# The twelve pairs of a combined input projection in another order: values, gates and queries first

## Chip, cores and metric

One core of one Trainium2 chip runs the whole program in one launch. The metric is device time in microseconds (us), the median of three runs. Engines are named as the profile names them: PE (TensorE), DVE (VectorE), ACT (ScalarE), POOL (GpSimd), SP (SyncE, which issues most DMA transfers).

## What is computed

Two layers of a streaming encoder for a sequence of 1024 frames, 1024 channels. Each layer normalises its input, makes one projection of it whose columns are shared out to three mixers, joins their outputs in one output projection with a residual add, and ends in a gated feed-forward net (FFN) with a width-3 convolution and another residual add. Cut to the parts around the change:

```python
q, k = rotary(q, pos) * 64 ** -0.5, rotary(k, pos)   # retention: 4 heads, uses q, k, v, g
xbc = silu(causal_dwconv(xbc, conv_w, conv_b))        # SSD: 512 + 2*128 + 2*128 columns, width 4
y_ssd = groupnorm(ssd_scan(xbc, dt) * silu(z))
xc = causal_dwconv(xin, conv_w, conv_b)               # RG-LRU: width 4
r, i = sigmoid(xc @ w_a + b_a), sigmoid(xc @ w_x + b_x)
a = exp(-8 * r * softplus(-lam)); u = sqrt(1 - a * a) * (i * xc)
h_t = a_t * h_(t-1) + u_t                             # a scan over the frames
y_lru = h * gelu(gate)
```

Retention works with a decaying state over chunks, the SSD mixer with a state of 128 per head over chunks; all inputs and outputs are float32.

## The kernel before

Time is cut into two halves of HT = 512 frames; channels lie on the 128 partitions. A product in float32 is made of three products of split numbers: an operand is split into a rounded high part (ACT, a copy) and the rest (DVE, a subtraction, or POOL, an accumulating DMA): `part_split`, lines 235 to 243, for weights, and L206 for the input.

The input projection of a layer has 24 column tiles of 128. Two neighbouring tiles form a *pair* (class Pair), and a pair's two tiles times two halves, four products of 1024 by 128 by 512, are made with seven smaller products of sums and differences (Strassen's scheme in Winograd's form). `prep` (L851) makes the sums of the weights with four operations (L710: a11, s2, a21, a12) and splits the five results. A pair behind the first then has 84 matmuls on L300, 24 in `start` and 60 in `end`, in five groups of twelve; each group ends in additions (L874, L879, L882, L883, L886), of which L890 is the pair's last. L837 is the addition in `start`. In layer 0 the additions of `start` are followed by L847 and L848, a multiplication by the norm's factors. In front, L744 to L750 are the normalising multiplications of the input itself.

`ORDER` (line 46) names the twelve pairs of a layer in the order in which they are made; both layers use it. A name such as x:6 is a kind and the first tile of the pair. `products` (L895) makes the first pair with `lead` and `follow`, starts the next two early, while the input is still being normalised and split, and then makes one pair after another. Small products for the step sizes dt (L413 is a DVE operation in it) follow pair 1 and pair 3. When a part of a pair is ready, `take` in `in_pair` (L938) hands it on:

- x (four pairs: x:0, x:2, x:4, x:6): `xbc` (L387), a convolution (L315 on ACT, three L318 on DVE), a tanh on ACT, L393, and a store to DRAM;
- z (two pairs) and g: `silu2` (L340), a tanh on ACT and L344 on DVE, and a store;
- v: a store alone;
- q and k: `rotate` (L372), four small DMAs that swap rows (L377) and two that load tables (L381, tile tb), L382, L383, L384 on DVE, and a store;
- lru (two pairs): the first tile goes through `gelu2` (L331, DVE L335, L336, L338), the second through `lru` (L346): a convolution, two gate products on PE (tile lgp, L353), tanh, exp and a square root on ACT (L354 to L360; tables are exchanged for the square root), DVE's L359 and L361, POOL's L362, the scan L363, POOL's L366, and a store.

Each step of this list is done four times for a pair (two tiles, two halves), the recurrence of lru twice. While one pair's results are taken, PE makes the next pair.

Behind the last pair come the `mixers` (L634): in eight chunks of 128 frames they load what was stored (L643), run the SSD chunk (L535; L547 and L575 multiply by masks, cumb is a tile of decays that is loaded by L566, L558 and L559 are POOL's products), the retention chunk (L427) and the gates; and then the output projection (tile op, its products also on L300) and the FFN. Weight splits of the output projection (w_o) are also made there.

A scheduling framework lays the instructions into each engine's queue from the order in which the code is written and an estimate of when each can run, so one engine's rows of several pairs are mixed. The queue is then worked through in order.

Of the kernel before, what the change touches and what calls it, by code (L numbers as in the profile page):

```python
# [42 lines left out]

ORDER = tuple((n, int(i)) for n, i in (x.split(":") for x in "q:0 x:6 z:0 x:2 x:4 lru:0 lru:2 z:2 x:0 k:0 g:0 v:0".split()))
PLACE = {"x": 0, "z": 8, "lru": 12, "k": 16, "q": 18, "g": 20, "v": 22}


# [1 line left out]
def hybrid_trunk(  # L51
# [29 lines left out]
    def nm(s):  # L81
        uid[0] += 1
        return f"{s}{uid[0]}"
# [46 lines left out]
    for k in range(2 * KD):  # L130
# [3 lines left out]
        if k in (1, 5):  # L134
            r = wr.tile([P, 2 * HT], F32, tag="wr", name=nm("wr"))
            (sp, act)[(k + 1) % 2].dma_start(r, w_ct[0, PLACE[ORDER[0][0]] + ORDER[0][1] + len(first) - 1])
            first.append(r)
# [800 lines left out]
    def in_pair(l, kind, i, B):  # L938

        g0 = PLACE[kind] + i  # L940
        gl = {}

        def take(m, h, x, then=None):
            if kind == "x":
                xbc(l, h, i + m, x, then)
                return
            if kind == "lru" and m:
                lru(l, h, i // 2, x, gl[h], then)
                return
            x = body(x)  # L950
            if kind in "zg":
                silu2(x)
                keep(l, h, kind, i + m, x)
            elif kind == "v":
                keep(l, h, kind, i + m, x)
            elif kind in "qk":
                rotate(l, h, kind, i + m, x)
            else:
                gelu2(x)
                gl[h] = x  # L960

        return Pair((w_ct[l, g0], w_ct[l, g0 + 1]), B, take)
# [249 lines left out]
    for l in range(DEPTH):  # L1212
# [15 lines left out]

        pairs = [in_pair(l, kind, i, B) for kind, i in ORDER]
        if l:  # L1230
# [181 lines left out]
```

## Time and profile before

| | us |
|---|---|
| runs | 2347.9, 2351.53, 2354.42 |
| median of the runs | 2351.53 |
| the profiled execution's own time | 2346.2 |
| its span in the trace | 2344.4 |
| PE busy | 2174.7 (93%) |
| DVE busy | 1924.6 (82%) |
| ACT busy | 1288.4 (55%) |
| POOL busy | 302.6 (13%) |

Busy times are those of one profiled execution; a line such as L300 is a line of the kernel, and a helper's line stands for all that call it. Layer 0's projection runs from the start to about 342 us, its mixers to 424, layer 1's projection from about 1200 to 1486 and its mixers to 1567.

### The profile page before, as it was taken

Reading aid. Unit: us, or ns where it says so; the run is one execution under the profiler, and the core shown is the slowest. Engines: PE = TensorE matmul, PEld = TensorE weight load, DVE = VectorE, ACT = ScalarE, POOL = GpSimd, SP = SyncE. Lnnn points to the kernel's source line nnn. Section 1 sums busy time; section 2 is a strip of 40 time slices with the busy share of each in tenths; the row PEclk is TensorE's granted clock in tenths of the full one; section 3 lists DMA queues with packets and bytes.
Section 4 is the critical chain, followed back from the end, with each engine's and each line's share of the span. In section 5 each row is a group of like instructions: output and inputs, shape, how many; then the busy total and the mean of one; then the engine's idle time right before and its main releaser. Section 6 shows DMA issues by size and latency. Waiting matters only on the chain.

```text
span 2344.4 us, 31562 instructions
## 1 busy us (share of the span) xinstructions
PE 2174.7 (93%) x10494; PEld 1758.3 (75%) x10494; DVE 1924.6 (82%) x3763; ACT 1288.4 (55%) x2370; POOL 302.6 (13%) x335
## 2 busy tenths in 40 slices
PE   6699988997999999999978989899989999999997
PEld 4477767885788888878866767777668888887787
DVE  7987858779877788999798877696797788789987
ACT  5357637554566556444445674674556665654443
POOL 0012213000222222000001131210002222210000
PEclk9799999999999999999988999999989999999999
DMA  4365687561666666854334638846437666677522
GB/s 173 108 149 134 150 248 233 167 209 48 149 150 148 145 153 152 285 193 137 108 128 123 152 79 235 266 150 208 137 93 164 144 148 148 147 197 254 178 83 73
DMA packets 176147, 371.94 MB, mean 159 GB/s; under 512 B 19440, under 2 KB 31856, under 8 KB 175984
## 3 DMA queue, kind: packets, MB, share of 16 engines
q1 hardware_dynamic: 135760, 297.55, 38.6%
q0 software_dynamic: 37440, 68.17, 17.1%
q10 hardware_dynamic: 2784, 4.20, 0.5%
q8 instruction: 83, 1.36, 0.3%
q14 instruction: 80, 0.66, 0.1%
HBM read 228.22 MB, written 69.27 MB: 127 GB/s over the span
## 4 chain that ended last, share of the span: by engine, by line
PE 65%; DVE 15%; DMA 8%; issue 7%; ACT 3%; SPq 1%; POOL 1%; DVEq 0%; POOLq 0%; ACTq 0%
PE up L300 43%; PE op L300 6%; PE dy L995 5%; PE dx L995 5%; PE dx L1071 2%; DMA ws<-wr 2%; DVE ws L243 2%; DVE bl L206 1%; DVE xb L318 1%; DMA cumb<-cumscr 1%; DMA tb<-in_rope_dram 1%; DMA g<-g1scr 1%; DMA g<-g0scr 1%; DVE g L710 1%; DMA wr<-in_w_ct_dram 1%
## 5 line engine op out<-in xcount | busy, mean ns | idle before, releaser
L300 PE MATMUL up<-bh,ws 128*128 128x512 f32 x3840 | 1228.2, 400 | 76.4 <-ACT ws L236 50.5
L300 PEld LDWEIGHTS up<-bh,ws 128*128 128x128 f32 x3840 | 735.6, 192 | 249.7 <-ACT ws L236 54.0
L300 PE MATMUL up<-bl,ws 128*128 128x512 f32 x1920 | 761.1, 398 | 11.8 <-DVE bl L206 11.7
L236 ACT ACTIVATE ws<-wr 128x512 fp32r<-128x512 f32 x568 | 348.7, 626 | 358.9 <-PE up L300 129.0
L300 PEld LDWEIGHTS up<-bl,ws 128*128 128x128 f32 x1920 | 369.2, 192 | 102.3 <-DVE bl L206 22.4
L241 POOL DMA_DIRECT2D ws<-wr x222 | 197.6, 905 | 1321.5 <-ACT ws L240 1046.0
L243 DVE TENSOR_TENSOR ws<-wr,ws 128x512 fp32r<-128x512 f32 x346 | 236.5, 688 | 61.0 <-ACT ws L236 54.9
L995 PE MATMUL dy<-ws,ws 128*128 128x512 f32 x792 | 192.2, 390 | 3.2 <-ACT ws L236 1.6
L995 PE MATMUL dx<-ws,ws 128*128 128x512 f32 x792 | 190.8, 390 | 2.1 <-ACT ws L236 1.2
L995 PEld LDWEIGHTS dy<-ws,ws 128*128 128x128 f32 x792 | 148.2, 188 | 36.4 <-DVE ws L243 3.3
L995 PEld LDWEIGHTS dx<-ws,ws 128*128 128x128 f32 x792 | 148.4, 188 | 34.1 <-ACT ws L236 2.1
L318 DVE SCALAR_TENSOR_TENSOR fc<-u,smalls,fc 128x512 f32<-128x512 f32 (+2 forms) x176 | 131.0, 748 | 50.6 <-ACT fc L315 49.6
L240 ACT ACTIVATE ws<-ws 128x512 fp32r<-128x512 f32 x260 | 159.8, 626 | 4.6
L300 PE MATMUL op<-yh,ws 128*128 128x512 f32 x512 | 160.5, 394 | 0.2 <-ACT yh L213 0.2
L318 DVE SCALAR_TENSOR_TENSOR fc<-c,smalls,fc 128x512 f32<-128x512 f32 (+2 forms) x176 | 131.2, 745 | 0.7 <-ACT fc L315 0.3
L315 ACT ACTIVATE fc<-c,smalls 128x512 f32<-128x512 f32 x88 | 71.2, 809 | 103.7 <-DVE c L837 101.7
L243 DVE TENSOR_TENSOR ws<-g,ws 128x512 fp32r<-128x512 f32 (+1 forms) x165 | 103.1, 649 | 13.7 <-ACT ws L236 13.5
L236 ACT ACTIVATE ws<-g 128x512 fp32r<-128x512 f32 (+1 forms) x165 | 92.1, 590 | 39.7 <-PE dy L995 13.8
L300 PEld LDWEIGHTS op<-yh,ws 128*128 128x128 f32 x512 | 95.4, 188 | 21.7 <-ACT yh L213 2.1
L300 PE MATMUL op<-yl,ws 128*128 128x512 f32 x256 | 100.3, 394 | 0.0
L710 DVE TENSOR_TENSOR wr<-wr,wr 128x512 f32<-128x512 f32 x64 | 44.9, 702 | 63.0 <-DMA wr<-in_w_up_dram 28.3
L236 ACT ACTIVATE ws<-s 128x512 fp32r<-128x512 f32 x64 | 40.4, 632 | 101.3 <-DVE s L710 92.4
(303 smaller groups left out, 2939.3 us busy)
## 6 DMA issues: line engine op xcount, KB each, us to landing
ws<-wr POOLq DMA_DIRECT2D x222, 256.0 KB, 4.3
wr<-in_w_up_dram SPq DMA_DIRECT2D x96, 512.0 KB, 4.3
wr<-in_w_dn_dram SPq DMA_DIRECT2D x66, 512.0 KB, 3.9
wr<-in_w_ct_dram SPq DMA_DIRECT2D x56, 512.0 KB, 4.7
wr<-in_w_o_dram SPq DMA_DIRECT2D x32, 512.0 KB, 5.1
g0scr<-fc SPq DMA_DIRECT2D x44, 256.0 KB, 3.3
g<-g0scr SPq DMA_DIRECT2D x44, 256.0 KB, 5.8
g1scr<-fc SPq DMA_DIRECT2D x44, 256.0 KB, 2.9
```

The source lines that it names most:

```text
L206: eng.tensor_tensor(lo, src, hi.bitcast(F32), op=ALU.subtract)
L236: act.activation(w[:, 0, :m], raw, AF.Copy)
L240: act.activation(w[:, 1, :m], w[:, 0, :m].bitcast(F32), AF.Copy, scale=-1.0)
L241: pool.dma_start(w[:, 1, :m].bitcast(F32), raw, accum_op=ALU.add)
L243: eng.tensor_tensor(w[:, 1, :m], raw, w[:, 0, :m].bitcast(F32), op=ALU.subtract)
L300: pe.matmul(dst, W(k, a), A(k, b), start=first and i == 0, stop=last and i == n - 1)
L315: act.activation(dst, body(x), AF.Identity, bias=bias, scale=taps(n))
L318: dve.scalar_tensor_tensor(dst[:, o:HT], x[:, HALO - j + o : HALO - j + HT], taps(n - j), dst[:, o:HT], op0=ALU.mult, op1=ALU.add)
L710: eng.tensor_tensor(o, a, b, op=op)
L995: pe.matmul(d[oc], w[:, a, P * oc : P * oc + P], t[:, b], start=not more and i == 0 and k == 0, stop=i == NP - 1 and k == 2, skip_group_ch ...
L1071: pe.matmul(X[oc][:, e], w[x][:, P * oc : P * oc + P], t[:, y, e], start=False, stop=i == NP - 1 and k == 2, skip_group_check=True)
```

## The change

Line 46 gets another order of the same twelve names. Nothing else is edited; the preload of the first pair's weights (line 136) follows the first name by itself.

```diff
@@ -43,7 +43,7 @@
-ORDER = tuple((n, int(i)) for n, i in (x.split(":") for x in "q:0 x:6 z:0 x:2 x:4 lru:0 lru:2 z:2 x:0 k:0 g:0 v:0".split()))
+ORDER = tuple((n, int(i)) for n, i in (x.split(":") for x in "v:0 z:0 g:0 z:2 q:0 x:6 k:0 x:2 lru:0 x:4 x:0 lru:2".split()))
```

The first three pairs, which are made beside the normalising of the input, were q, x:6 and z:0 and are v, z:0 and g; the last three were k, g and v and are x:4, x:0 and lru:2. The two recurrent pairs stood sixth and seventh, and stand ninth and last.

What DVE has in its queue at the front of layer 0, behind the first products of the early pairs. Before (c and qs are q's output and its swapped copy, x and t the input and its sums):

```order
L320 COPY u_407<-c_421 128x3
L710 TENSOR_TENSOR t_752<-x_125,x_93 128x512
L750 SCALAR_TENSOR_TENSOR x_103<-x_103,first,nr_455 128x512
L382 TENSOR_TENSOR c_353<-c_353,tb_566 128x512
L383 TENSOR_TENSOR qs_561<-qs_561,tb_567 128x512
L206 TENSOR_TENSOR bl_755<-t_752,bh_754 128x512
L384 TENSOR_TENSOR c_353<-c_353,qs_561 128x512
L710 TENSOR_TENSOR x_103<-x_103,t_752 128x512
```

The same place now:

```order
L710 TENSOR_TENSOR t_699<-x_125,x_93 128x512
L344 SCALAR_TENSOR_TENSOR c_421<-gt_695,c_421 128x512
L750 SCALAR_TENSOR_TENSOR x_103<-x_103,first,nr_455 128x512
L206 TENSOR_TENSOR bl_702<-t_699,bh_701 128x512
L710 TENSOR_TENSOR x_103<-x_103,t_699 128x512
```

The rotation's three operations are gone from between the input's sums and splits, and one L344 (of z) stands there.

What DVE has in its queue ahead of the last pair's weights in layer 0 (wr and s are the raw weights and their sums, the row that writes s is the s2 subtraction). Before, with g's last additions around v's weights:

```order
L710 TENSOR_TENSOR wr_2622<-wr_2622,wr_2665 128x512
L879 TENSOR_TENSOR u_2564<-u_2490,up_2551 128x512
L710 TENSOR_TENSOR s_2668<-wr_2665,wr_2622 128x512
L882 TENSOR_TENSOR u_2490<-u_2490,up_2567 128x512
L883 TENSOR_TENSOR c_2565<-u_2564,up_2567 128x512
L886 TENSOR_TENSOR u_2490<-u_2490,up_2582 128x512
L890 TENSOR_TENSOR u_2564<-u_2564,up_2600 128x512
L243 TENSOR_TENSOR ws_2670<-s_2668,ws_2670 128x512
```

Now, with x:0's convolutions (xb) around lru:2's weights, all of it behind x:0's L890:

```order
L318 SCALAR_TENSOR_TENSOR xb_2547<-u_2493,smalls,xb_2547 128x509
L320 COPY c_2494<-u_2493 128x3
L837 TENSOR_TENSOR c_2602<-u_2588,up_2575 128x512
L393 SCALAR_TENSOR_TENSOR xb_2525<-u_2414,xb_2525 128x512
L393 SCALAR_TENSOR_TENSOR xb_2547<-u_2493,xb_2547 128x512
L318 SCALAR_TENSOR_TENSOR xb_2556<-c_2494,smalls,xb_2556 128x512
L847 TENSOR_TENSOR c_2602<-c_2602,nr_455 128x512
L318 SCALAR_TENSOR_TENSOR xb_2556<-c_2494,smalls,xb_2556 128x512
L848 TENSOR_TENSOR u_2588<-u_2588,nr_455 128x512
L318 SCALAR_TENSOR_TENSOR xb_2556<-c_2494,smalls,xb_2556 128x512
L335 TENSOR_SCALAR lt_2606<-lt_2606 128x512
L710 TENSOR_TENSOR s_2615<-wr_2612,wr_2564 128x512
```

The s2 subtraction stood four rows ahead of the previous pair's last addition, and stands behind it and behind the three convolutions that follow it.

What DVE has in its queue at the seam from the last pair to the mixers in layer 0 (cbt and cumb are chunk masks and decays of the SSD mixer). Before:

```order
L890 TENSOR_TENSOR u_2717<-u_2717,up_2750 128x512
L547 TENSOR_TENSOR cbt_2790<-cb_2787,mats 128x256
L575 TENSOR_TENSOR cumb_2811<-cumb_2811,cbt_2790 128x512
L575 TENSOR_TENSOR cumb_2828<-cumb_2828,cbt_2790 128x512
L547 TENSOR_TENSOR cbt_2892<-cb_2889,mats 128x256
L575 TENSOR_TENSOR cumb_2913<-cumb_2913,cbt_2892 128x512
```

Now:

```order
L890 TENSOR_TENSOR u_2664<-u_2664,up_2702 128x512
L338 SCALAR_TENSOR_TENSOR u_2588<-lt_2696,u_2588 128x512
L320 COPY c_2665<-u_2664 128x3
L547 TENSOR_TENSOR cbt_2790<-cb_2787,mats 128x256
L318 SCALAR_TENSOR_TENSOR xc_2716<-u_2664,smalls,xc_2716 128x511
L575 TENSOR_TENSOR cumb_2811<-cumb_2811,cbt_2790 128x512
L318 SCALAR_TENSOR_TENSOR xc_2716<-u_2664,smalls,xc_2716 128x510
L575 TENSOR_TENSOR cumb_2828<-cumb_2828,cbt_2790 128x512
L318 SCALAR_TENSOR_TENSOR xc_2716<-u_2664,smalls,xc_2716 128x509
L361 SCALAR_TENSOR_TENSOR xc_2716<-ti_2722,xc_2716 128x512
L318 SCALAR_TENSOR_TENSOR xc_2742<-c_2665,smalls,xc_2742 128x512
L359 SCALAR_TENSOR_TENSOR lv_2730<-u_2664,lv_2730 128x512
```

The masks of chunk 1 (cbt_2892 and its cumb tiles) stood four rows behind the last addition, and stand some twenty rows behind it, with the recurrent pair's operations and some splits of w_o between.

## Rows read from the trace of the kernel before

**Rows 1.** The page, busy time of each engine, share of the span and instructions.

```profile
PE 2174.7 (93%) x10494; PEld 1758.3 (75%) x10494; DVE 1924.6 (82%) x3763; ACT 1288.4 (55%) x2370; POOL 302.6 (13%) x335
```

**Rows 2.** Busy times by stretch; the first line names the columns.

```profile
core 0: us, PE busy (x) PEld busy (x) DVE busy (x) ACT busy (x) POOL busy (x), PEclk, DMA share, GB/s
590.00:960.00 370.00, 370.00 (x1626) 306.13 (x1625) 298.08 (x498) 223.27 (x362) 75.94 (x88) 0.99 0.65 155
...
60.00:100.00 40.00, 30.48 (x103) 19.64 (x101) 39.58 (x66) 10.83 (x18) 0.00 (x0) 0.83 0.43 138
...
1220.00:1260.00 40.00, 22.91 (x90) 16.73 (x89) 36.30 (x61) 17.15 (x30) 0.86 (x1) 0.74 0.33 99
...
342.00:424.00 82.00, 71.11 (x781) 62.77 (x779) 72.79 (x265) 61.00 (x186) 26.01 (x22) 1.00 0.64 209
```

**Rows 3.** Timeline of PE: start, us, instruction, [idle before <-releaser].

```profile
109.28 0.60 PE L418 MATMUL dtt<-mats,dtc 16*128 16x16 f32 x4 [10.02 <-DVE dtc L413]
...
240.00 3.78 PE L353 MATMUL lgp<-xc,mats 128*128 128x512 f32 x4 [3.80 <-DVE xc L318]
...
1240.40 0.80 PE L300 MATMUL up<-bh,ws 128*128 128x512 f32 x1 [17.09 <-ACT ws L236]
```

**Rows 4.** Timeline of DVE at the two fronts, same columns.

```profile
100.79 4.05 DVE L318 SCALAR_TENSOR_TENSOR xb<-u,smalls,xb 128x512 f32<-128x512 f32 x6
...
1201.14 0.69 DVE L744 TENSOR_TENSOR xd<-xd,rows 128x512 f32<-128x512 f32 x1 [2.08 <-ACT rows L736]
...
1240.81 0.68 DVE L206 TENSOR_TENSOR bl<-xd,bh 128x512 fp32r<-128x512 f32 x1
1241.41 0.68 DVE L243 TENSOR_TENSOR ws<-s,ws 128x512 fp32r<-128x512 f32 x1
```

**Rows 5.** DVE, last additions: z:0, x:2, lru:0, x:0, v; layer 1: z:0, lru:0, x:0, v.

```profile
132.62 0.68 DVE L890 TENSOR_TENSOR u<-u,up 128x512 f32<-128x512 f32 x1
...
153.53 0.68 DVE L890 TENSOR_TENSOR u<-u,up 128x512 f32<-128x512 f32 x1
...
193.47 0.68 DVE L890 TENSOR_TENSOR u<-u,up 128x512 f32<-128x512 f32 x1
...
270.75 0.68 DVE L890 TENSOR_TENSOR u<-u,up 128x512 f32<-128x512 f32 x1
...
342.07 0.69 DVE L890 TENSOR_TENSOR u<-u,up 128x512 f32<-128x512 f32 x1 [1.03 <-PE up L300]
...
1279.71 0.68 DVE L890 TENSOR_TENSOR u<-u,up 128x512 f32<-128x512 f32 x1
...
1338.57 0.68 DVE L890 TENSOR_TENSOR u<-u,up 128x512 f32<-128x512 f32 x1
...
1417.00 0.68 DVE L890 TENSOR_TENSOR u<-u,up 128x512 f32<-128x512 f32 x1
...
1485.65 0.69 DVE L890 TENSOR_TENSOR u<-u,up 128x512 f32<-128x512 f32 x1 [1.25 <-PE up L300]
```

**Rows 6.** Timeline of DVE, a rotation of k in layer 0.

```profile
300.39 0.69 DVE L382 TENSOR_TENSOR u<-u,tb 128x512 f32<-128x512 f32 x1 [5.52 <-DMA tb<-in_rope_dram]
```

**Rows 7.** Chain that ended last: start, us, what; output projections of both layers.

```profile
424.02 2.51 PE op L300 x10
...
1566.86 2.96 PE op L300 x12
```

**Rows 8.** Timeline of ACT (table load), of POOL and of DVE in the mixers.

```profile
204.23 1.28 ACT L360 ACT_TABLE_LOAD   x1 [0.94 <-DVE lv L359]
205.53 0.72 ACT L360 ACTIVATE lv<-lv,tiny 128x512 f32<-128x512 f32 x1
...
406.75 1.04 POOL L558 TENSOR_TENSOR xd<-xtc,dd 128x512 f32<-128x512 f32 x1 [5.24 <-PE cb L554]
...
406.82 2.97 DVE L575 TENSOR_TENSOR cumb<-cumb,cbt 128x512 f32<-128x512 f32 x2
...
368.22 1.28 DVE L575 TENSOR_TENSOR cumb<-cumb,cbt 128x512 f32<-128x512 f32 x2
```

## The prediction

> **What bounds the kernel now.** I read the page first: over its span of 2344.4 us PE is busy 2174.7 us, 93%, and DVE 1924.6, 82% [rows 1]. So what can be won is the time in which PE waits, and the table by stretch shows where that is. From 590 to 960 us (the FFN) PE is busy all of 370.00 us, 1626 matmuls, 0.2276 us each [rows 2]; ORDER does not touch that. PE is short of work at the projection's front in layer 0 (60 to 100: PE 30.48 of 40, DVE 39.58 of 40), at its front in layer 1 (1220 to 1260: PE 22.91, DVE 36.30), and in the mixers (342 to 424: PE 71.11, DVE 72.79 of 82) [rows 2]. At both fronts DVE is the bound, since PE's long waits there end on DVE's work or the split that follows it: 10.02 us until the dt step's add, 17.09 us before layer 1's first products with w2 [rows 3].
>
> Next, the middle. A pair behind the first has 84 matmuls, 84 x 0.2276 = 19.1 us at full speed. From pair 2's last add (L890) to pair 11's are nine pairs, 172 us, but layer 0 takes 342.07 - 132.62 = 209.5 and layer 1 1485.65 - 1279.71 = 205.9 [rows 5]. The loss sits in few places. From lru:0's end to x:0's, three pairs of which one is lru:2, are 270.75 - 193.47 = 77.3 and 1417.00 - 1338.57 = 78.4 for 57.3: 20.0 and 21.1 more. Two pairs' recurrences do their work in that stretch (a pair's outputs are finished under the next), so **10.0 and 10.6 us for one recurrent pair**; one such stop is the gate matmul that waits 3.80 us for the convolution and takes 3.78 [rows 3]. From x:0's end to v's, again three pairs, are 71.3 and 68.7: 14.0 and 11.4 more, of which I give k's rotation 10 and 8 (DVE waits up to 5.52 us for a rotation's table [rows 6]) and the end of the layer about 4.
>
> **The change, part by part.** Only the order of twelve pairs changes; all instructions stay. "Per layer" below is layer 0 / layer 1.
>
> *Front.* Counted up to the dt step's add, DVE in layer 0 has twelve rotation operations, eleven convolution steps (L318) and three L393 less, and four L344, an L848 and a subtraction more. Plain operations start 0.60 us apart (1240.81, 1241.41 [rows 4]), six convolution steps take 4.05, so some 0.67 each: -12 x 0.60 - 11 x 0.67 - 3 x 0.60 + 6 x 0.60 = **-12.8**. PE waits for exactly this end (10.02 us), and the rest speeds the starved stretch ahead of it. In layer 1 DVE goes from its first normalising multiply at 1201.14 to the split of s2 at 1241.41, 40.3 us [rows 4]; the changed order has 42 rows there, 42 x 0.60 = 25.2, with s2's three subtractions moved ahead of the stretch. So up to 15.1 earlier, against a wait of 17.09. The splits on ACT and the products that PE makes ahead of this wait need not end sooner, so I take **-11**, with 8 to 15 as bounds. q's swap and table transfers also leave the front of SP's queue, where the weight loads then stand sooner; nothing there is on PE's path in the rows, so nought.
>
> *lru:2 leaves the middle* for the last place: its 10.0 / 10.6 go from there: **-10.0 / -10.6**. lru:0 stays.
>
> *x:6 enters the middle* in place of g or v. The first x pair behind z:0 took 153.53 - 132.62 = 20.9, 1.8 above 19.1 [rows 5]; layer 1's were at most 1 above: **+1.8 / +0.3**.
>
> *q's rotation enters the middle.* In front DVE was full while it ran (39.58 of 40 [rows 2]), so it hardly waited for its transfers. Bounds: nought, and what k's costs, 10 / 8. In the changed order k's s2 subtractions stand ahead of most of q's twelve operations, so PE's weights are not behind the table. I take **+4 / +4**, nearer to the lower end.
>
> *Late preparation of the last pairs.* A pair's first 24 matmuls (24 x 0.2276 = 5.5 us) cover its s2 subtraction and split. Counting DVE's rows, before, the subtraction stands ahead of the previous pair's L890 nearly everywhere; now lru:2's stands 10.9 us of DVE work behind it in layer 0 and x:0's 13.0 in layer 1, behind x:0's (x:4's) convolutions. With a split behind the subtraction (ACT's copy and a subtraction like that of 1241.41 [rows 4], some 0.7 each), 10.9 + 1.4 - 5.5 = 6.8 and 13.0 + 1.4 - 5.5 = 8.9 of waiting; some 4 of it replaces the old end's loss: **+3 / +4** rounded, 0 to 9.
>
> *lru:2 in the mixers.* Its convolutions, gates and scans now stand between the first chunks' operations. DVE's rows in that stretch grow by six L318, two each of L361, L359 and L363 and one L338, about 8.1 us, in layer 1 7.4. The mixers take from v's L890 to the first products of the output projection, 424.02 - 342.07 = 82 and 1566.86 - 1485.65 = 81 [rows 5, 7], with DVE busy 72.79 of layer 0's 82 [rows 2], so 9 idle. Bounds: +4 (half of the work falls into that idle time) and +20 (below). I take the added DVE work itself, **+8 / +7**: what holds add and what idle time takes up cancel. On ACT four table loads move there with it, each 1.28 us [rows 8], so 4 x 1.28 = 5.1; ACT has more idle time than DVE, so that is in the upper bound alone. The Trainium skill ("ScalarE: Activation LUTs", What ACT_TABLE_LOAD costs) puts a drain of about 1.38 us beside each load, which would make it an estimated 10.6; the trace here shows the load's own 1.28 and 1.30 from its start to that of the next operation [rows 8], no drain; by the page the ACT work moved would be 5 us a layer more, and the sum is left as it is.
>
> Sum, layer 0: -12.8 - 10.0 + 1.8 + 4 + 3 + 8 = **-6.0**. Layer 1: -11 - 10.6 + 0.3 + 4 + 4 + 7 = **-6.3**. Together -12.3. The profiled execution took 2346.2, so 2333.9; the runs' median lies 5.3 above it, so **2339**, 0.5% less. A difference under about 0.3% (7 us) can't be told from none.
>
> **Rivals.**
> *More is won.* The mixers take up half of lru:2 (+4), q's rotation costs 1, and no preparation is late (0). Then -12.8 - 10.0 + 1.8 + 1 + 4 = -16.0 and -11 - 10.6 + 0.3 + 1 + 4 = -16.3: 2351.5 - 32.3 = **2319**. For it: in the old order v came last, and v's store, its load and the loads queued behind it on SP opened the mixers; now all of that is done earlier. Against it: DVE is full in the mixers' later part.
>
> *Nothing is won.* q's rotation costs what k's does, 10 / 8 in place of 4 / 4: -6.0 + 6 = 0 and -6.3 + 4 = -2.3: **2349**. For it: every rotation of k waited on a table [rows 6]; against it, the order of rows named above.
>
> *Slower: the mixers are held up by lru:2.* Chunk 1's mask multiplies (L575) now stand behind twenty or so rows in DVE's queue, some of them waiting for ACT's square root or POOL's product, and in POOL's queue chunk 2's products stand behind the second half's L362. The price: 8.1 of DVE work, 3.6 for the six w_o splits that now stand among those rows, 3.5 for table loads, and POOL. A mask multiply pair took 2.97 us beside POOL's product and 1.28 without one [rows 8]. Four products of lru:2, each holding DVE about 1.3, are up to 5. Together 20 in place of 8 / 7: +12 and +13, so 2339 + 25 = **2364**. It decides once the mixers grow by more than some 14 us a layer. The Trainium skill ("GPSIMD Engine Reference", 1. Specifications) says that GpSimd shares its SBUF interfaces with VectorE and contends with instructions that have two SBUF inputs; the two rows agree, and by that rule this rival's last 5 us would be owed in full.
>
> **How the numbers follow.** Chances: the forecast 0.35, more is won 0.25, nothing 0.20, slower 0.20. The front and lru:2's leaving (-44 together) are read from rows; the costs (+32) are my choices between bounds. Faster by over 0.3%: most of the forecast (0.27) and nearly all of the second (0.24): 0.51. Within 0.3%: 0.08 of the forecast, 0.16 of nothing, a little from the others: 0.28. Slower: 0.21. The range reaches from a little below the case of more (2316) to the slower case (2364), which leaves out half of the one's lower and of the other's upper side, about 2 in 10. All lower bounds together would give -17.0 and -21.3, 2313, just outside; the mixers' upper bound with the other choices kept is the upper end.
>
> **What would show it.** Front: the wait before L413's reader falls from 10.02 to under 3, and layer 1's 17.09 to about 6. Middle: from pair 2's L890 to pair 11's about 195 to 200 in both layers. Four tables' waits of q may appear; PE should have no gap over 3 us there save before the last pair, 3 to 9. Mixers: 88 to 90 from the last L890 to the first output product; 86 or less speaks for the second case, 96 and more for the slower. The prediction is wrong if the time saved in front comes back as waits of the same size in the middle.

## The result

The changed kernel takes 2410.84 us (2408.1 to 2412.87) against 2349.82 of the kernel before: ratio 1.0256, interval 1.0235 to 1.0277, 61 us slower. 2339 was forecast, with 2364 as the upper end. The span of its profiled execution is 2410.8 us, 66.4 more than before's.

The page of the changed kernel, busy time of each engine:

```profile
PE 2195.4 (91%) x10494; PEld 1771.4 (73%) x10494; DVE 1935.9 (80%) x3763; ACT 1288.9 (53%) x2370; POOL 304.7 (13%) x335
```

All engines run as many instructions as in [rows 1]. DVE is busy 11.3 us longer with them and ACT 0.5; PE's same 10494 matmuls keep it busy 20.7 us longer, and the rest of the 66 us is time in which PE waits. The table by stretch of the changed kernel (columns as in [rows 2]): the two fronts, then middle and mixers of layer 0, and of layer 1:

```profile
60.00:100.00 40.00, 29.96 (x111) 20.63 (x112) 38.22 (x65) 12.57 (x21) 0.00 (x0) 0.88 0.22 79
1220.00:1260.00 40.00, 37.04 (x169) 28.47 (x167) 38.52 (x76) 20.96 (x37) 0.00 (x0) 1.00 0.35 119
119.50:357.50 238.00, 190.62 (x776) 151.05 (x775) 165.56 (x277) 111.29 (x200) 38.07 (x41) 0.89 0.66 176
357.50:462.40 104.90, 82.13 (x790) 68.21 (x789) 89.08 (x286) 73.26 (x199) 31.95 (x26) 0.92 0.42 126
1304.40:1531.00 226.60, 185.50 (x772) 147.41 (x770) 155.22 (x267) 110.46 (x198) 37.12 (x41) 0.92 0.65 167
1531.00:1636.70 105.70, 83.78 (x789) 70.67 (x789) 85.12 (x276) 72.96 (x199) 30.55 (x26) 0.90 0.50 163
```

The middles of the kernel before, the same view, for comparison:

```profile
132.60:342.00 209.40, 187.08 (x771) 147.51 (x771) 159.77 (x278) 119.39 (x208) 43.11 (x46) 0.95 0.65 168
1279.70:1485.70 206.00, 187.82 (x783) 148.62 (x782) 150.10 (x257) 120.53 (x209) 42.52 (x46) 0.96 0.66 170
```

In the middles PE's busy time hardly changes (187.08 and 190.62, 187.82 and 185.50), so nearly all that was added there is time in which PE waits. In layer 0's mixers PE's busy time rose from 71.11 [rows 2] to 82.13 us, at a granted clock of 0.92 instead of 1.00 and with lru:2's gate products among its work. The last additions on DVE of the changed kernel, against [rows 5]: layer 0's g, k, x:2, lru:0, x:4, x:0, lru:2, then layer 1's g and lru:2:

```profile
119.55 0.68 DVE L890 TENSOR_TENSOR u<-u,up 128x512 f32<-128x512 f32 x1
...
209.39 0.68 DVE L890 TENSOR_TENSOR u<-u,up 128x512 f32<-128x512 f32 x1
...
240.18 0.68 DVE L890 TENSOR_TENSOR u<-u,up 128x512 f32<-128x512 f32 x1
...
268.26 0.69 DVE L890 TENSOR_TENSOR u<-u,up 128x512 f32<-128x512 f32 x1 [0.27 <-PE up L300]
...
303.50 0.67 DVE L890 TENSOR_TENSOR u<-u,up 128x512 f32<-128x512 f32 x1
...
319.98 0.67 DVE L890 TENSOR_TENSOR u<-u,up 128x512 f32<-128x512 f32 x1
...
357.54 0.69 DVE L890 TENSOR_TENSOR u<-u,up 128x512 f32<-128x512 f32 x1 [0.18 <-PE up L300]
...
1304.42 0.68 DVE L890 TENSOR_TENSOR u<-u,up 128x512 f32<-128x512 f32 x1
...
1530.95 0.68 DVE L890 TENSOR_TENSOR u<-u,up 128x512 f32<-128x512 f32 x1
```

| stretch | before | after | difference | forecast |
|---|---|---|---|---|
| start to pair 2's last add, layer 0 | 132.6 | 119.6 | -13.1 | -12.8 |
| middle, layer 0 | 209.5 | 238.0 | +28.5 | -1.2 |
| mixers, layer 0 | 81.9 | 104.8 | +22.9 | +8 |
| FFN, and front of layer 1 | 855.8 | 842.1 | -13.7 | -11 |
| middle, layer 1 | 205.9 | 226.5 | +20.6 | -2.3 |
| mixers, layer 1 | 80.1 | 104.7 | +24.5 | +7 |

The mixers here run from the last L890 to the output projection's first product of a low part, so that all kernels are measured alike; what lies behind them changed by under 4 us. The fronts came out in time as worked out. The middles and the mixers gave it back more than three times over.

The two longest waits of PE in layer 0's middle, and two behind them (timeline of PE, changed kernel):

```profile
243.09 0.80 PE L300 MATMUL up<-bh,ws 128*128 128x512 f32 x1 [15.91 <-ACT ws L236]
...
333.53 0.79 PE L300 MATMUL up<-bh,ws 128*128 128x512 f32 x1 [13.96 <-ACT ws L236]
...
343.89 1.22 PE L300 MATMUL up<-bh,ws 128*128 128x512 f32 x2 [5.55 <-DMA ws<-wr]
...
373.79 3.76 PE L353 MATMUL lgp<-xc,mats 128*128 128x512 f32 x4 [6.20 <-DVE xc L318]
```

The first stands under x:2, behind k's rotation, ahead of lru:0's weights; the second ahead of lru:2's weights; the last is lru:2's gate product in the mixers. What DVE does ahead of the first (its timeline: k's rotations, then lru:0's s2 subtraction):

```profile
217.35 0.69 DVE L382 TENSOR_TENSOR u<-u,tb 128x512 f32<-128x512 f32 x1 [6.68 <-DMA tb<-in_rope_dram]
...
223.07 0.69 DVE L382 TENSOR_TENSOR u<-u,tb 128x512 f32<-128x512 f32 x1 [3.36 <-DMA tb<-in_rope_dram]
...
231.25 0.69 DVE L382 TENSOR_TENSOR c<-c,tb 128x512 f32<-128x512 f32 x1 [2.73 <-issue]
...
240.78 0.68 DVE L710 TENSOR_TENSOR s<-wr,wr 128x512 f32<-128x512 f32 x1
```

And what SP's queue issues there:

```profile
208.90 0.32 SPq L370 DMA_DIRECT2D kscr<-c  x1
209.53 4.30 SPq L377 DMA_DIRECT2D qs<-u  x4
213.93 1.02 SPq L381 DMA_DIRECT2D tb<-in_rope_dram  x2
215.06 2.41 SPq L377 DMA_DIRECT2D qs<-u  x4
219.74 0.33 SPq L370 DMA_DIRECT2D kscr<-u  x1
220.11 0.93 SPq L381 DMA_DIRECT2D tb<-in_rope_dram  x2
221.09 2.42 SPq L377 DMA_DIRECT2D qs<-c  x4
226.63 0.33 SPq L370 DMA_DIRECT2D kscr<-u  x1
227.00 0.93 SPq L381 DMA_DIRECT2D tb<-in_rope_dram  x2
228.04 0.84 SPq L781 DMA_DIRECT2D wr<-in_w_ct_dram  x2
```

This is the loop to see: the store of one rotation (219.74) can go only when DVE has made it (L384 at 219.02); the next rotation's tables (220.11) stand behind that store; DVE waits for them until 223.07; and so on once more at 226.63, 227.00 and 231.25 (for this last wait, 2.73 us, the trace names no releaser). The weights of a later pair (228.04) stand behind all of it. DVE, which waits for tables, holds x:2's additions and convolutions and lru:0's s2 subtraction behind its waiting instruction, and PE, which has made its products, waits 15.91 us.

### The profile page after: what moved, and what is told of

It reads as the page before. It is cut to its first block, busy times and chain, and to the rows that moved or that the text cites. A ratio compares the mean times of both kernels' runs of the same rounds, so it can differ in the third digit from the quotient of the medians.

```text
span 2410.8 us, 31620 instructions
## 1 busy us (share of the span) xinstructions
PE 2195.4 (91%) x10494; PEld 1771.4 (73%) x10494; DVE 1935.9 (80%) x3763; ACT 1288.9 (53%) x2370; POOL 304.7 (13%) x335
## 5 line engine op out<-in xcount | busy, mean ns | idle before, releaser
L300 PE MATMUL up<-bl,ws 128*128 128x512 f32 x1920 | 763.7, 399 | 10.1 <-DVE bl L206 10.0
L243 DVE TENSOR_TENSOR ws<-wr,ws 128x512 fp32r<-128x512 f32 x346 | 238.0, 693 | 65.4 <-ACT ws L236 62.1
L243 DVE TENSOR_TENSOR ws<-g,ws 128x512 fp32r<-128x512 f32 (+1 forms) x165 | 103.1, 649 | 12.6 <-ACT ws L236 12.3
```

What stands on the lines that cost most here:

```text
L243: eng.tensor_tensor(w[:, 1, :m], raw, w[:, 0, :m].bitcast(F32), op=ALU.subtract)
L300: pe.matmul(dst, W(k, a), A(k, b), start=first and i == 0, stop=last and i == n - 1)
```

## Experiments

A ratio is to the kernel before, measured beside the run. That kernel took 2341 to 2350 us over all these runs, so times of different runs can be compared to some 8 us only; the lengths of stretches are those of one profiled execution of each.

**The last place: e1 and e2.**

```diff
 e1:  q:0 x:6 z:0 x:2 x:4 lru:0 lru:2 z:2 x:0 k:0 g:0 v:0      (before)
-> q:0 x:6 z:0 x:2 x:4 lru:0 z:2 x:0 k:0 g:0 v:0 lru:2
 e2:  v:0 z:0 g:0 z:2 q:0 x:6 k:0 x:2 lru:0 x:4 x:0 lru:2      (changed)
-> v:0 z:0 g:0 lru:2 q:0 x:6 k:0 x:2 lru:0 x:4 x:0 z:2
```

> The order of before with lru:2 alone moved to the last place. Theory A (the mixers pay for a recurrent pair in the last place, whatever stands ahead of it): from the last L890 to the output products 82 and 81 us become about 104 and 105; the middle gets some 10 us a layer back; so about +13 a layer, 2350 + 26 = 2376. Theory B (the mixers of the changed kernel are long because x:0 and x:4 come late, ahead of lru:2): the mixers grow by the added DVE work alone, 8 a layer, and the time is 2350 - 4 = 2346.

2376.87 us, ratio 1.0120 (1.0098 to 1.0141). Mixers 106.3 and 108.6 us, middles 200.7 and 194.3 (8.8 and 11.6 less). Theory A in each number.

> The changed order with z:2 and lru:2 exchanged, so that a light pair is last and the recurrent pair fourth. Theory A: the mixers go back to 82 to 86 in both layers (-40 in all) and the 13.96 us wait ahead of the last pair goes; the fourth pair pays about 10 a layer: 2411 - 40 - 20 + 20 = about 2370. Theory B: the mixers stay above 98, 2395 or more.

2402.8 us, 1.0239 (1.0221 to 1.0257). The mixers fell to 86.8 and 79.9, as A says; but the middles grew to 247.0 and 240.4. The recurrence as fourth pair now falls under q, whose pair took 38.1 and 34.2 us instead of 23.5 and 23.2. So the price of the last place is shown twice, and the time of A was wrong: a recurrence ahead of a rotation cost 14.6 and 11.1, more than the 10 us that I took. The wait ahead of the last pair, which was to go, stayed (timeline of PE, e2, layer 0, ahead of z:2's weights):

```profile
345.16 0.80 PE L300 MATMUL up<-bh,ws 128*128 128x512 f32 x1 [11.33 <-ACT ws L236]
```

So most of it belongs to the last place, behind x:0's convolutions, and not to lru:2.

**The rotations: e4, f1, e5, f2, e6.**

```diff
 e4 (changed order) and f1 (order of before):
             elif kind in "qk":
-                rotate(l, h, kind, i + m, x)
+                keep(l, h, kind, i + m, x)
 e5 (changed order), in rotate:
-        tb = [t_tile("tb") for _ in range(2)]
-        ...
-                sp.dma_start(tb[j], rope[2 * tab + j, :, HT * h : HT * h + HT])
-        dve.tensor_tensor(x, x, tb[0], op=ALU.mult)
-        dve.tensor_tensor(sw, sw, tb[1], op=ALU.mult)
+        one = ones[:, 0:1].to_broadcast([P, HT])
+        dve.tensor_tensor(x, x, one, op=ALU.mult)
+        dve.tensor_tensor(sw, sw, one, op=ALU.mult)
 f2 (changed order):
-                sp.dma_start(tb[j], rope[...])
+                act.dma_start(tb[j], rope[...])
 e6 (changed order), in up_raw:
-        sp.dma_start(r[:, : 2 * HT], src)
+        act.dma_start(r[:, : 2 * HT], src)
```

> The changed kernel without the rotations: q and k are stored as they come from the projection (their swaps, tables and the 24 DVE operations a layer are left out). Theory A: what the two rotations cost in the middle goes, 13 and 20 us in layer 0 and about as much in layer 1: 238 and 227 us between the last additions become about 205 and 200, the time about 2411 - 60 = 2350. Rival D (they cost their DVE work alone, 24 x 0.60 = 14 us a layer where DVE is the bound, and the middle is lost to convolutions and late weights instead): 2411 - 15 = 2395 or more.

2342.97 us, 0.9982 (0.9969 to 0.9995), 68 less than the changed kernel (64 by the ratios). Middles 202.2 and 196.1, so 35.8 and 30.5 less.

> The kernel before without the rotations (q and k stored as projected), the counterpart of the changed kernel without them (2343). Theory A (the rotations' price hangs on their place: q's in front costs 2 to 7 a layer, k's in the middle about 10): about 2346 - 30 = 2316, so that the rotations cost 30 before and 68 after. Rival K (they cost the same anywhere, and what was lost is something else): about 2280.

2320.97 us, 0.9896 (0.9880 to 0.9912), 24 less than before; middles 198.2 and 197.7, so 11.3 and 8.2 less. Theory A: the same rotations cost 24 us in one order and 64 to 68 in the other. The 24 are a net figure: the fronts were shorter too, but from the last L890 to the FFN's first last addition this run took 8.7 and 9.3 us more than the kernel before, which was not looked into. The middles are the cleaner comparison. Without rotations the two orders' middles are alike (202.2 and 198.2, 196.1 and 197.7).

> The changed kernel with its rotations, but without the two table loads of each (the multiplications take a column of ones that is resident, so the rotated values differ): swaps, DVE operations and stores stay. Theory T (DVE waits for tables, which stand in SP's queue behind stores that wait for DVE, and need free temporary tiles): most of what the run without rotations won is won here too, 45 of 68, so about 2365. Theory S (the swaps and stores in SP's queue, with the weight loads behind them, are enough by themselves): 2395 or more.

2380.57 us, 1.0130 (1.0111 to 1.0150), 30 less than the changed kernel; middles 222.9 and 205.5, so 15.1 and 21.1 of the 35.8 and 30.5. Between T and S: about half of the rotations' price goes with the tables; the rest stays with the swaps, stores and operations, which no run separates.

> The changed kernel with the rotations' table loads issued from ACT's queue instead of SP's, nothing left out. Theory T (tables wait in SP's queue behind stores that wait for DVE): most of what the run without tables won (30 us) is won, 2380 to 2390. Rival U (the tables wait for free temporary tiles, or for their transfer, whichever queue issues them): 2403 or more.

2379.89 us, 1.0146 (1.0129 to 1.0163). That is 31 less than the changed kernel (26 by the ratios). Nothing is left out, and the middles are 227.9 and 205.7, so 10.1 and 20.8 less, against the 15.1 and 21.1 that leaving the tables out had won. So most of what the tables cost is where they stand in SP's queue, not their transfer: theory T. A rotation of q in that run (timeline of DVE):

```profile
168.64 0.69 DVE L382 TENSOR_TENSOR u<-u,tb 128x512 f32<-128x512 f32 x1 [6.43 <-DMA qs<-u]
```

What DVE waits for now is the swap, which SP's queue issues from 161.64 on, as soon as DVE has made its source (L886, 160.93 to 161.61).

> The changed kernel with the weight loads of all pairs issued from ACT's queue instead of SP's, in both the projection and the FFN. Theory S: weights no longer wait behind q's and k's stores, the wait of 15.91 us under lru:0 and the s2 subtractions' waits for weights go: about 20 us a layer less in the middle, 2370. Theory V (DVE's own queue holds the s2 subtraction behind the rotation's operations, whatever the weights do): no more than 8 a layer, 2395 or more; a time above 2411 would say that ACT's queue is held up by the loads.

2396.49 us, 1.0203 (1.0183 to 1.0223); middles 234.4 and 215.6, so 3.6 and 11.0 less. Nearest to V: weights behind the stores are a part, some 7 us a layer, and by f2 the tables that DVE waits for are a larger one in both layers.

**What makes the recurrence dear in the mixers: e7, e8, e9**, all on the order of e1.

```diff
 e7:
-            gp = s_bank("lgp")
-            pe.matmul(gp, wg[l, n][:, i, :], xc, start=True, stop=True)
-            act.activation(t, gp, AF.Tanh, ...)
+            act.activation(t, xc, AF.Tanh, ...)
 e8:
-        act.activation(v, v, AF.Sqrt, bias=tiny, scale=0.0625)
+        act.activation(v, v, AF.Square, bias=tiny, scale=0.0625)
 e9:
-        pool.tensor_tensor(xc, xc, v, op=ALU.mult)
+        dve.tensor_tensor(xc, xc, v, op=ALU.mult)
-        pool.tensor_tensor(ti, ti, gl, op=ALU.mult)
+        dve.tensor_tensor(ti, ti, gl, op=ALU.mult)
```

> The order of before with lru:2 last, without the gate products of the recurrent pairs (the two tanh read the convolution itself, so the gates' values differ). Theory P (the gate products stand in PE's queue ahead of the chunks' products and wait there for the convolution, 2.38 and 5.72 us, and PE then works at the lower clock): the mixers' 106 and 109 fall to about 90, the time to about 2377 - 32 - 8 (the other recurrent pair) = 2337. Theory Q (DVE's and ACT's added work hold the mixers): 100 or more, 2360 or more.

2363.82 us, 1.0064 (1.0043 to 1.0085). Mixers 101.2 and 103.1, 5 less each: theory P falls. The gate products' wait is a part of the price, not the price.

> The order of before with lru:2 last, with a square in place of the square root, which needs no exchange of tables (the scan's input differs). Theory P: under 3 us a layer, 2371 or more. Theory A with table loads as a cause: four loads of 1.28 us stand ahead of what DVE and POOL wait for, 5 to 10 a layer, 2357 to 2367.

2371.22 us, 1.0085 (1.0065 to 1.0105). Mixers 102.4 and 103.1, 3.9 and 5.5 less; counted up to the FFN's first last addition, 1.0 and 4.6 less. A layer's four loads there are 4 x 1.28 = 5.1 us of ACT, and they cost about that or less.

> The order of before with lru:2 last, with the recurrent pairs' two products (L362, L366) on DVE instead of POOL. If POOL's queue and its hold on DVE are part of what the mixers lost (5 us a layer by the prediction's slower rival): mixers 101 to 103 instead of 106 and 109, about 2367. If not, DVE's four more operations cost 0 to 3 a layer: 2377 to 2383.

2376.33 us, 1.0134 (1.0117 to 1.0151). Mixers 107.3 and 110.7, 1 and 2 more, with four more operations a layer on DVE. POOL's products are at most a small cause: what moving them won is no more than what these operations cost.

In e1 itself, the first 40 us of layer 0's mixers (table by stretch; the second row is the kernel before in its first 24):

```profile
332.80:373.00 40.20, 26.30 (x176) 18.78 (x177) 29.45 (x63) 26.97 (x54) 14.14 (x12) 0.72 0.51 175
```

```profile
342.00:366.00 24.00, 21.91 (x241) 19.34 (x239) 19.16 (x57) 17.94 (x56) 10.27 (x9) 1.00 0.84 269
```

In 40 us PE makes 176 products where it made 241 in 24, none of the four engines is full (DVE 29.45, ACT 26.97 of 40.2), and the granted clock is 0.72. Two rows of PE's and three of ACT's timeline there show where they wait:

```profile
340.44 3.44 PE L353 MATMUL lgp<-xc,mats 128*128 128x512 f32 x4 [2.38 <-DVE xc L318]
...
349.61 3.78 PE L353 MATMUL lgp<-xc,mats 128*128 128x512 f32 x4 [5.72 <-DVE xc L318]
```

```profile
347.25 1.28 ACT L360 ACT_TABLE_LOAD   x1
...
351.76 1.28 ACT L354 ACT_TABLE_LOAD   x1 [1.46 <-PE lgp L353]
...
359.70 1.28 ACT L360 ACT_TABLE_LOAD   x1
```

The recurrence is one chain across PE, ACT, POOL and DVE, two halves of it one behind the other, from the convolution at 335 to the second half's last store at 366. The chunks' operations are laid into the same queues between its steps, and each step waits for another engine. The chain of work that ended last (view of the chain, e1) runs through it:

```profile
334.63 0.82 ACT xc L315
335.48 0.75 DVE xc L318
...
340.44 3.46 PE lgp L353 x4
343.92 0.69 ACT ti L354
...
349.61 3.78 PE lgp L353 x4
353.39 1.08 PE yd L562 x8
```

From 334.63 to 353.39 it names, but for two mask multiplies of 2.05 us, steps of the recurrence alone: 16.7 us of the 24.5 by which layer 0's mixers grew. Taking out a single link (gates 5, tables 4 to 5, POOL 0) shortens the mixers by that link alone; DVE's added operations are 8 by their rows. That is 17 to 18 of the 24.5 and 28.5 by which e1's mixers grew; the rest is not accounted for by one link. SP's queue, where the first half's store (354.35) is the first transfer after 340.1, is not the last link there: on the chain the next load of decays, at 355.24, follows PE's L580. No run moved these stores.

**Where lru:2 can stand: f3.**

```diff
-q:0 x:6 z:0 x:2 x:4 lru:0 lru:2 z:2 x:0 k:0 g:0 v:0
+q:0 x:6 z:0 x:2 x:4 lru:0 z:2 x:0 k:0 g:0 lru:2 v:0
```

> The order of before with lru:2 eleventh, ahead of v. If the recurrence is dear in the mixers because it falls into them (and not because it is late), one light pair of 19 us behind it takes most of it: mixers 84 to 92 instead of 106 and 109, the pair v pays 6 to 10 in the middle, time about 2346 to 2356. If the chain of one recurrence takes longer than a pair (two halves, some 15 us each in the run with lru:2 last), the mixers stay above 95 and the time above 2362.

2333.26 us, **0.9958 (0.9942 to 0.9974)**: 0.4% faster than the kernel before, and better than the first case had it; the middles, 205.3 and 198.3, are 4 and 8 us shorter than before's. Last additions of lru:2 and v in layer 0 (DVE), then lru:2's second gate product under v and the first product of the output projection's low part:

```profile
305.82 0.68 DVE L890 TENSOR_TENSOR u<-u,up 128x512 f32<-128x512 f32 x1
...
337.74 0.68 DVE L890 TENSOR_TENSOR u<-u,up 128x512 f32<-128x512 f32 x1
```

```profile
325.62 1.88 PE L353 MATMUL lgp<-xc,mats 128*128 128x512 f32 x4
...
416.77 0.48 PE L300 MATMUL op<-yl,ws 128*128 128x512 f32 x1
```

v's pair takes 31.9 us (27.3 in layer 1), 13 and 8 above 19.1, and the mixers are 79.0 and 81.6, as before. This gate product waits for nothing and takes 1.88 us, where the one at 349.61 in e1 waited 5.72 and took 3.78. One light pair behind the recurrence was enough.

**The front: n1, n2, e3, o2.**

```diff
-q:0 x:6 z:0 x:2 x:4 lru:0 lru:2 z:2 x:0 k:0 g:0 v:0
+q:0 k:0 z:0 x:2 x:4 lru:0 lru:2 z:2 x:0 x:6 g:0 v:0    (n1)
+q:0 g:0 z:0 x:2 x:4 lru:0 lru:2 z:2 x:0 k:0 x:6 v:0    (n2)
+z:0 x:6 g:0 x:2 x:4 lru:0 lru:2 z:2 x:0 k:0 q:0 v:0    (e3)
+v:0 q:0 g:0 x:2 x:4 lru:0 lru:2 z:2 x:0 x:6 k:0 z:0    (o2)
```

> The order of before with k and x:6 exchanged, so that both rotations are in the front and x:6 stands tenth. Theory F (in the front a rotation is nearly free, since DVE has other work while it waits, and what is dear there is the convolution; in the middle a rotation costs 10 to 17 us): front 5 to 11 less in layer 0 and 3 to 6 in layer 1, middle 10 and 8 less for k, 2 more for x:6: about 2350 - 28 = 2322. Rival G (twelve more DVE operations in a front where DVE is the bound cost 7 each layer and SP's queue holds the next weights): 2345 to 2360.

2348.17 us, 1.0009 (1.0000 to 1.0019): no difference. In the profiled execution, which was the fastest of ten (2339.3), layer 0's front was 1.9 shorter, the middles 4.6 and 11.5, but FFN and layer 1's front took 862.1 instead of 855.8. The time is G's, and so is layer 1's front; layer 0's is neither's. Rotations in front are not free in layer 1.

> The order of before with g and x:6 exchanged: q stays in the front, the convolution leaves it and stands eleventh, ahead of v. Theory F: the front's gain of the changed order (13 a layer) came from x:6 leaving, so pair 2's last add of layer 0 stands at about 121 instead of 132.6 and layer 1's 10 sooner; x:6 costs 2 to 4 a layer behind k: 2350 - 17 = about 2333. Theory H (the front's gain came from q's rotation leaving): pair 2's end above 128, 2345 to 2355.

2353.33 us, 1.0038 (1.0025 to 1.0051). Layer 0's pair 2 ended at 126.7, 5.9 sooner, between F and H: of the 13 us that the change won there, x:6's leaving is about 6, and without q's rotation (f1) it ended at 125.6, 7 sooner. Behind k, x:6 took 28.5 and 26.3 and v 30.2 and 26.2.

> The order of before with q taken out of the front alone: z:0 and g:0 stand first and third, q stands eleventh behind k and ahead of v. Theory A (a rotation in the middle holds up SP's queue and with it the weights of the pairs behind it): the front gains some 7 a layer, q's rotation costs 10 to 14 a layer as k's does: 2350 - 14 + 24 = 2360. Rival C (only rotations with x pairs behind them are dear): q's rotation costs under 4 a layer, and the time is 2340 to 2346.

2374.08 us, 1.0119 (1.0094 to 1.0145), worse than A had it. The front won 2 in layer 0, and 9 in layer 1 (301.4 us from the FFN's last L890 to pair 2's instead of 310.4). The middles took 219.5 and 213.8, 10.1 and 7.9 more: behind k and with only v behind it, q's rotation costs what k's does, and rival C falls. q's and v's pairs took 31.3 and 29.9 in layer 0 where g's and v's had taken 26.3 and 22.2. From the last L890 to the FFN's first last add were 249.5 and 255.9 instead of 240.5 and 241.3, which neither theory had.

> An order put together from the runs: v, q and g in front (no convolution there, q's rotation where it is cheap), the recurrent pairs where they were, x:6 between x:0 and k, z:0 last. By the parts measured: front 6 less in layer 0 and 0 to 5 in layer 1, x:6 dearer by 1 a layer, the end as before: about 2335 to 2340. If a light pair in front is worth nothing once q is there, 2346.

2364.32 us, 1.0076 (1.0060 to 1.0093): wrong by 24 and more. The front of layer 0 won 5, and layer 1's mixers took 99.2 where layer 0's took 84.4 with the same order. Counted up to the FFN's first last add both layers lost, 12.7 and 18.4 us from the last L890 on. The parts did not add up, and why z:0 last costs that was not looked into further.

**Both findings together: g1, g2.**

```diff
 order of f3, and in rotate:                              (g1)
-                sp.dma_start(tb[j], rope[...])
+                act.dma_start(tb[j], rope[...])
 order:                                                   (g2)
+q:0 k:0 z:0 x:2 x:4 lru:0 z:2 x:0 x:6 g:0 lru:2 v:0
```

> The order of before with lru:2 eleventh, and the tables issued from ACT's queue. If both findings hold together: k's rotation, about 10 a layer in the middle, loses half of its price, 2333 - 10 = 2323. If q's rotation in front now holds ACT's queue, or k was held by its swaps alone, 2330 or more.

> Both rotations in front, x:6 tenth or ninth, lru:2 eleventh ahead of v. If the parts add up (both rotations in front won 0 to 7, lru:2 eleventh 11): 2326 to 2334. If x:6 behind x:0 makes lru:2's weights late, 2340 or more.

g1 2333.84 us, 0.9963 (0.9950 to 0.9976); g2 2334.13, 0.9965 (0.9949 to 0.9981). Neither is better than f3: with g behind k the tables' place in a queue made no difference (g1's middles are 204.0 and 199.3, f3's 205.3 and 198.3), and rotations in front again won nothing.

## Why the prediction was wrong

*The front* was right in time: -13.1 and -13.7 for -12.8 and -11. PE's product behind the dt step, which had waited 10.02 us at 109.28 [rows 3], comes 10.9 us sooner and still waits 4.18, where under 3 had been expected (timeline of PE, changed kernel):

```profile
98.37 0.60 PE L418 MATMUL dtt<-mats,dtc 16*128 16x16 f32 x4 [4.18 <-DVE dtc L413]
```

Layer 1's 17.09 became three of 2.2 to 3.0.

*lru:2 leaving the middle* was right: e1, which does this alone, won 8.8 and 11.6 for 10.0 and 10.6.

*q's rotation enters the middle* (+4, with k's 10 and 8 as upper bound) **is the step that failed first**. The rotations' price in the middle rose from 11.3 and 8.2 (f1 against before) to 35.8 and 30.5 (e4 against the changed kernel), 24.5 and 22.3 more where 4 and 4 were forecast. That is 20.5 and 18.3 of the 29.7 and 22.9 us by which the middles missed their forecast; the other 9.2 and 4.6 lie in the remaining terms. Two things were wrong in the term for q. I read DVE's order alone, found k's subtractions ahead of q's operations and was content. Of SP's queue I counted what left the front ("nought") and not what came into the middle: stores that wait for DVE, the next tables behind them (f2: 26 to 31 us), and the weights of later pairs (e6: 12 to 14 us). And I took k's 10 and 8 as its own price and left it unchanged, though the pairs behind it were light ones (g, v) before and are x:2 and lru:0 now. Against e4, the pairs q and x:6 took 12.7 and 12.6 us more, above the bounds of 10 and 8, and the pairs from k to lru:2 took 23.1 and 18.0 more, where k's rotation had cost 11.3 and 8.2 with the light pairs. So the term for q was short by 8.7 and 8.6, and k's move, which had no term at all, cost 11.8 and 9.8. In layer 0, x:2 and lru:0 took 30.8 and 28.1 with rotations and 22.1 and 19.5 without, and x:6 behind q 28.5 and 19.0. The price read in [rows 6] was therefore no bound for another place; with light pairs behind q (e3) it holds, 10.1 and 7.9.

*x:6 in the middle* (+1.8, +0.3): 19.0 and 19.0 where no rotation stands ahead of it (e4), so no dearer than 19.1.

*Late preparation* (+3, +4) had the right place in layer 0 and too small a size. In the run without rotations, PE still waits for lru:2's weights in layer 0 (timeline of PE, e4):

```profile
297.90 0.79 PE L300 MATMUL up<-bh,ws 128*128 128x512 f32 x1 [10.45 <-ACT ws L236]
```

With 5.56 more for a split made by the accumulating DMA these waits come to 16.0, where 6.8 had been worked out, and that pair takes 36.3, 17.2 above 19.1. What I left out: the preparations behind s2 stand as late as s2, and the last weights of a pair go through ACT, POOL and a transfer. In layer 1 of that run PE has no wait above 4.2 us in the middle, so the 8.9 worked out for x:0 there does not show.

*lru:2 in the mixers* (+8, +7) is the step that failed second: +22.9 and +24.5, above the upper bound of 20. Taking the added DVE work as the price was wrong in kind. No engine is full in the first 40 us of e1's mixers; the recurrence is a chain across four engines, and 16.7 us of the chain that ended last are its links. Which rows carry the rest stays open. The slower rival had the place, the point from which it decides, and nearly the size. Of its parts the table loads were about right (3.9 and 5.5 for 3.5), POOL's hold on DVE did not show (e9).

*Chances.* The slower rival alone would have been 2364. It came together with a worse form of the rival in which nothing is won, and I had treated the two as alternatives, each with the other's terms at their forecast. They are different places, so a case with both belonged in the range; by the prediction's own sizes it would have been 2364 + 10 = 2374, still 37 us short of the result.

## What to carry to other kernels

A step that issues transfers is moved in every queue that it uses: at its new place, write down what stands behind its stores and loads in the queue that issues its transfers, and behind its waiting operation on the engine, and price those. A loss that the trace shows behind a step belongs to the step and its followers together; it is no bound once the followers change. A long chain across several engines wants a piece of independent work behind it that keeps PE busy; here one light pair made the difference between 24 to 28 us more in the mixers and none, and became 13 and 8 us longer itself.

## What the runs showed of the hardware

The exchange of ACT's tables cost about what the loads last. Four a layer fell into e1's mixers, 1.28 us each, and without them the mixers were 3.9 and 5.5 us shorter (e8). The Trainium skill ("ScalarE: Activation LUTs", What ACT_TABLE_LOAD costs) gives 2.66 us for every switch, load and drain together, an estimated 10.6 for four. The trace shows the load without the drain: 1.28 us, and ACT's next operation 1.30 after its start (347.25 and 348.55 in e1).

A wait of PE cost a second time here. Where lru:2's gate product comes behind 5.72 us without work in e1, its four matmuls take 3.78 us (granted clock 0.53 from 349 to 354, so mostly the lower level, 1.2 GHz); in f3, where PE has products of a pair around it, the four take 1.88 (granted clock 1.00 from 324 to 328, the upper level, 2.4 GHz).

Moving POOL's products of the recurrence to DVE won nothing that shows in the time (e9), though a pair of mask multiplies had taken 2.97 us beside another POOL product and 1.28 without [rows 8]. In e1's layer 0 the mask multiplies did not meet the recurrence's products: the pair at 355.42 took 1.29 us, and POOL's L366 had ended at 354.31. The Trainium skill ("GPSIMD Engine Reference", 1. Specifications) states that GpSimd's SBUF interfaces are shared with VectorE and contended for by DVE instructions with two SBUF inputs. The two rows of [rows 8] agree with it; e9 is no test of it.
